# Softmax division moved from the attention weights to the attention outputs, with the reciprocals turned through DRAM

## The chip, the core and the metric

The kernel runs on one core of a Trainium2 chip. The core has five engines with one instruction queue each: TensorE (PE in the profile; its weight loads are listed apart as PEld), VectorE (DVE), ScalarE (ACT), GpSimd (POOL) and SyncE (SP), which here only starts DMAs. The metric is the device time of one execution in microseconds (us). Lower is better. Times of a kernel are medians of several runs; the profile is of one execution of its own.

## What is computed

The reference is one encoder layer over 1024 prompt tokens and, with the same weights, 512 sample tokens: RMS norm, neighbourhood attention, residual, RMS norm, a SwiGLU block, residual, final RMS norm. The change lies in the attention, which cut to what matters is:

```python
# per query row r, for each of 4 column blocks of 16 queries (x 8 rows in the kernel)
s = einsum('bjqhd,bkjchd->bhjqkc', qr, kr) * scale        # 16 heads of 64
s = where(valid, s + bias, -inf)
p = softmax(s)                                            # over the keys of the window
o = einsum('bhjqkc,bkjchd->bjqhd', p, vr)
y = o @ w_o
```

Softmax is exp(s - max) divided by the sum of these over the keys. The division can be done on the weights p, before they are multiplied with the values v, or on the outputs o, after it: the sum belongs to a query and a head, and the product with v is linear.

## The kernel before

Everything is float32. A product of two operands a and b is made of three TensorE passes over two-part splits (high part in a reduced format, low part the remainder), so each operand is cast once on ACT (`split`, L141) and its remainder subtracted on DVE (L142, or L144 and L145 where a scale is applied).

The attention runs over 8 head pairs. For the prompt a head pair takes 4 *steps* (two groups of 512 queries, two halves of each), for the sample 2 steps: 32 steps and then 16. A step works on two column blocks u = 0, 1 of 128 queries each and on both heads h of the pair. Function `step` (L477) traces its parts in this order:

1. `scores` (L391): for each block, 6 TensorE matmuls into two PSUM tiles `pss` (L397); on DVE the bias is added and the maximum taken (L405, `mx`); on ACT exp with the sum over keys as a side result `sm` (L408). DVE then takes the reciprocal `ri` (L410), and the weights `s`, 128 queries on the partitions by 384 keys (256 in the sample), are scaled by it: for h = 0 on DVE (L412), for h = 1 on ACT (L414).
2. `fill(0)`: a piece of other TensorE work, the projections of q and k for the next head pair (`pg`, L335) and, in the sample stage, pieces of the output projection (`pgo`, L593).
3. For the step before: `weighted` (L431, `po`, L434) multiplies the transposed weights `pT` with v, keys being contracted; the result lies with the 64 head dimensions on the partitions and the queries along the free axis. `collect` (L438) adds the two parts of the result, which lie in different partitions and columns of PSUM: a copy on ACT (L444) and two additions on DVE (L445, L447), the last of which writes `oT`. When both halves of a group are there, GpSimd's queue stores `oT` to DRAM (`o_d`, L462).
4. `flip` (L418), for each block: TensorE transposes the weights (`ptt`, L423) so that the keys lie on the partitions, ACT casts them to `pT` (L426), DVE subtracts for the low part (L427). After each, another `fill`.

After a step come up to two *chores* (class `Chores`, L166): a chore takes a raw tile that was loaded earlier (`rpool`, 2 buffers of tag `raw`), splits it with ACT and DVE, and starts the next load. The raw tiles are values (`vr`, four DMAs on SP's queue each, L381), weights of q and k (`wr`, L150), and later attention outputs. Bias tiles `b` (3 buffers) are filled two ahead: a memset on GpSimd (L207, L211) and DMAs on SP (L208, L209, L212, L213; L218 in the sample stage).

The order on each engine's queue is made at compile time by a planner: it takes instructions by their place in the program, but only those that its cost model holds ready at that time, so that an engine's order can differ from the program's. At run time each queue runs in order and waits at its head.

PSUM tiles of tag `S` (4 buffers) are shared by scores, transposes and others; tag `V` (2 buffers) holds `po`. Pool `apool` (L328) has 2 buffers for a tag unless it is said otherwise.

Of the kernel before, what the change touches and what calls it, by code (L numbers as in the profile page):

```python
# [11 lines left out]
F32 = mybir.dt.float32  # L12
F32R = mybir.dt.float32r
AF = mybir.ActivationFunctionType
ALU = mybir.AluOpType
# [3 lines left out]
P = 128  # L19
# [7 lines left out]
HP = H // 2  # L27
HD = 64
# [27 lines left out]
def body(tc, xp, xs, g_mix, g_ffn, g_fin, w_qkv, rpb, w_o, w_g, w_u, w_d, yp, ys):  # L56
    nc = tc.nc
# [8 lines left out]
    with es:  # L66
        cpool = es.enter_context(tc.tile_pool(name="cpool", bufs=1))
        stat = es.enter_context(tc.tile_pool(name="stat", bufs=4))
        ps = es.enter_context(tc.tile_pool(name="ps", bufs=2, space=PSUM))
        dr = es.enter_context(tc.tile_pool(name="dr", bufs=1, space=DRAM))  # L70
# [4 lines left out]

        v_d = [dr.tile([T, D // 2], F32, name=f"v_d{n}") for n in range(2)]
        o_d = dr.tile([HP, P, T], F32, name="o_d")
        x1_d = dr.tile([T, D], F32, name="x1_d")
        t_d = dr.tile([3, H, 16, 15, 32], F32, name="t_d")
        ti_d = dr.tile([3, H, 16, 15, 32], F32, name="ti_d")  # L80
# [29 lines left out]
        def psum(tag, name):  # L110
            return ps.tile([P, 512], F32, tag=tag, name=name, bufs=4 if tag == "S" else 2)
# [54 lines left out]
        class Chores:  # L166
# [7 lines left out]
            def fill(self):  # L174
                while self.jobs and len(self.loaded) < 2:
                    load, work = self.jobs.pop(0)
                    self.loaded.append((load(), work))
# [8 lines left out]
        def pool(name, **kw):  # L186
            cm = tc.tile_pool(name=name, **kw)
            return cm, cm.__enter__()
# [56 lines left out]
        with tc.tile_pool(name="vpool", bufs=2) as vp:  # L245
# [53 lines left out]
            for t in range(NT):  # L299
                if t + 2 < NT:  # L300
                    norm_tile(t + 2)
                if t == 0:
                    for td in (t_d, ti_d):
                        nc.sync.dma_start(
                            out=td.rearrange("k h i r c -> (k h i) (r c)").rearrange("(a p) f -> p a f", p=P),
                            in_=fill.rearrange("p (a f) -> p a f", a=1).to_broadcast([P, 6, 480]))
# [5 lines left out]
                if t == 8:  # L312
# [4 lines left out]
                              in_=t_d.rearrange("k h i r c -> (k h i) r c")[:, 3:11, :])  # L317
            for t in range(NT):
                v_tile(1, t, wv)
                q = t // 3  # L320
                half, src, st, n, dst = ((0, t_d, 7 - q, 8, es_d), (0, ti_d, 3 - q, 12, in_d),
                                         (4, t_d, 3 - q, 8, es_d))[t % 3]
                nc.gpsimd.dma_start(out=dst[:, :, half + q].rearrange("k h i f -> (k h) i f"),
                                    in_=src[:, :, :, st:st + n, :].rearrange("k h i r c -> (k h) i (r c)"))
# [3 lines left out]
        a_cm, ap = pool("apool", bufs=2, reuse_waits="tile")  # L328
# [59 lines left out]
            split(rv, vv[:, :, 0:4:3, :], vv[:, :, 1:3, :])  # L388
            return v

        def scores(q, k, krow, nrow, j, bias):  # L391
            n = nrow * 32
            pss = [psum("S", "pss") for _ in range(2)]
            for i, (a, b) in enumerate(PASS):
                for h, pt in enumerate(pss):
                    kv = k[h * HD:(h + 1) * HD, b].rearrange("p (r c) -> p r c", c=GW)
                    nc.tensor.matmul(pt[:, :n], q[h * HD:(h + 1) * HD, a, j].rearrange("p r i -> p (r i)"),  # L397
                                     kv[:, krow:krow + nrow, BS[j]:BS[j] + 32],
                                     start=(i == 0), stop=(i == 2))
            yield  # L400
            out = []
            for h, pt in enumerate(pss):
                s = ap.tile([P, 384], F32, tag="s", name="s", bufs=4)
                mx = stat.tile([P, 1], F32, tag="mx", name="mx")
                nc.vector.tensor_tensor_reduce(s[:, :n], pt[:, :n], bias(h), -1.0, 3.0e38,  # L405
                                               ALU.add, ALU.min, accum_out=mx)
                sm = stat.tile([P, 1], F32, tag="sm", name="sm")
                nc.scalar.activation(s[:, :n], s[:, :n], AF.Exp, bias=mx, scale=-1.0, accum_out=sm)  # L408
                ri = stat.tile([P, 1], F32, tag="ri", name="ri")
                nc.vector.reciprocal(ri, sm)  # L410
                if h == 0:
                    nc.vector.tensor_scalar(s[:, :n], s[:, :n], ri, None, ALU.mult)  # L412
                else:
                    nc.scalar.mul(s[:, :n], s[:, :n], ri)  # L414
                out.append(s)
            yield out

        def flip(ss, n):  # L418
            out = []
            for s in ss:  # L420
                pt = psum("S", "ptt")
                for c in range(n):
                    nc.tensor.transpose(pt[:, c * P:(c + 1) * P], s[:, c * P:(c + 1) * P], ident)  # L423
                pT = ap.tile([P, 3, 2, P], F32R, tag="pT", name="pT", bufs=4)
                pv = pt[:, :n * P].rearrange("p (c q) -> p c q", q=P)
                nc.scalar.copy(pT[:, :n, 0], pv)  # L426
                nc.vector.tensor_tensor(pT[:, :n, 1], pv, f32(pT[:, :n, 0]), ALU.subtract)  # L427
                out.append(pT)
            return out

        def weighted(pT, vs, j, n, pos, g):  # L431
            for h in range(2):
                for c in range(n):
                    nc.tensor.matmul(pos[h][:, g * 256:(g + 1) * 256], vs[c][:, j, h * P:(h + 1) * P],  # L434
                                     pT[h][:, c].rearrange("p z q -> p (z q)"),
                                     start=(c == 0), stop=(c == n - 1))

        def collect(pos, dst):  # L438
            for h in range(2):
                m, o = (0, HD) if h == 0 else (HD, 0)  # L440
                pv = pos[h].rearrange("p (g z q) -> p g z q", g=2, z=2)
                tmp = ap.tile([P, 2, P], F32, tag="tmp", name="tmp")
                t = tmp[m:m + HD]
                nc.scalar.copy(t, pv[o:o + HD, :, 0])  # L444
                nc.vector.tensor_tensor(t, t, pv[m:m + HD, :, 0], ALU.add)  # L445
                tv = t.rearrange("p g (r i) -> p g r i", i=16)
                nc.vector.tensor_tensor(dst(h), tv, pv[m:m + HD, :, 1].rearrange("p g (r i) -> p g r i", i=16),  # L447
                                        ALU.add)

        def steps(hp, g, q, k, v, n, store):  # L450

            oT = ap.tile([P, 512], F32, tag="o", name="oT", bufs=2)
            ov = oT.rearrange("p (r j i) -> p j r i", r=8, j=NJ)
            b = None
            for jj in range(2):
                sc = []
                for j in (jj * 2, jj * 2 + 1):
                    if j != 2:
                        b = next_bias()
                    sc.append(lambda b=b, j=j: scores(q, k, 4 * (g == 1), 4 * n, j, lambda h: b[:, h, :n * P]))  # L460
                yield dict(s=sc, n=n, jj=jj, v=v, dst=lambda h, jj=jj: ov[h * HD:(h + 1) * HD, jj * 2:jj * 2 + 2],
                           done=(lambda: nc.gpsimd.dma_start(out=o_d[hp, :, g * 512:(g + 1) * 512], in_=oT))  # L462
                           if jj else None)
                fill_bias()
# [10 lines left out]
        prev = []  # L475

        def step(st, fill):  # L477

            sc = [x() for x in st["s"]] if st else []
            for x in sc:  # L480
                next(x)
            ss = [next(x) for x in sc]
            fill(0)
            if prev:
                p, pT = prev.pop()
                pos = [psum("V", "po") for _ in range(2)]
                for u in range(2):
                    weighted(pT[u], [x() for x in p["v"]], p["jj"] * 2 + u, p["n"], pos, u)
                collect(pos, p["dst"])
                if p["done"]:  # L490
                    p["done"]()
            pT = []
            for u, x in enumerate(ss):
                pT.append(flip(x, st["n"]))
                fill(1 + u)
            if st:
                prev.append((st, pT))

        def drain(fillers):
            while fillers:  # L500
# [38 lines left out]
        for hp in range(HP):  # L539
# [5 lines left out]
            q0, q1, k = qk  # L545
# [10 lines left out]
            i = 0  # L556
# [56 lines left out]
        for hp in range(HP):  # L613
# [5 lines left out]
            n = len(jobs[hp])  # L619
# [323 lines left out]
        rt_cm, rt = pool("rt", bufs=1, side="right", reuse_waits="tile")  # L943
# [74 lines left out]
        def x_tile(tt, half, d, tag="c", bufs=15):  # L1018
            t = rows(tt, half)
            x = lt.tile([P, 512], F32, tag=tag, name=tag, bufs=bufs)  # L1020
            nc.gpsimd.dma_start(out=x, in_=x1_d[t * P:(t + 1) * P, d * 512:(d + 1) * 512])
            return x
# [28 lines left out]
        for q in range(84):  # L1051
            m, tt, h = q // 12, q % 12 // 2, q % 2
            n = SEQ[m]
# [8 lines left out]
            a, b = HALF[h]  # L1062
# [16 lines left out]
            elif n == 5:  # L1079
# [4 lines left out]
                x = x_tile(tt, 1, 0, "x", 2)  # L1084
# [45 lines left out]
```

## Time and profile before

| | |
|---|---|
| median of three runs | 1830.18 us (1823.91 to 1831.17) |
| the profiled execution | 1828.39 us, of which the span from first to last instruction is 1826.6 us |
| granted TensorE clock, mean | 0.987 |
| steps of the prompt attention | from 180 us into the span to about 517 us |
| steps of the sample attention | from 517 us to about 728 us |
| then the rest of the output projection and the SwiGLU block | to 1826.6 us |

The profile names a line of the kernel, the engine, the operation, what is written from what (`out<-in`), the count, and what ended idle time before an instruction (`<-`). A busy PE is not PE at its peak, since matmuls are pipelined and their ends are modelled. The rows that carry the argument are quoted where they are used.

### The profile page before, as it was taken

How to read it: one execution, taken by the hardware profiler on the slowest of the kernel's cores; microseconds unless marked ns; L12 is line 12 of the kernel's file. 1: busy time of each engine (PE TensorE's matmuls, PEld its weight loads, DVE VectorE, ACT ScalarE, POOL GpSimd, SP SyncE). 2: the span in 40 equal slices, each digit the busy share in tenths (PEclk: the TensorE clock that was granted, in tenths of full speed). 3: DMA queues.
4: the chain of work that ended last, by engine and by line, in shares of the span. 5: the costliest groups of instructions: out<-in, count | busy, mean ns of one | idle time of the engine just before them, and what ended most of it. 6: DMA issues, size and time to landing. Idle time of an engine off the chain costs nothing.

```text
span 1826.6 us, 25898 instructions
## 1 busy us (share of the span) xinstructions
PE 1755.7 (96%) x9178; PEld 1534.0 (84%) x9178; DVE 1222.2 (67%) x2263; ACT 869.9 (48%) x1742; POOL 441.4 (24%) x513
## 2 busy tenths in 40 slices
PE   7999999999999999999998999899999999999998
PEld 6887777777767878889998999899999988888886
DVE  4401887777887666667777877999777756546643
ACT  4411776767785554543443435433444435433423
POOL 1121000000130000103323343575424252005300
PEclk9999999999999999999999999899999999999999
DMA  7754333333465443643552635788343259645633
GB/s 242 220 187 157 108 108 101 104 117 108 125 203 155 139 145 121 196 162 120 173 167 93 209 107 168 257 295 287 112 136 122 78 191 322 194 153 165 215 103 107
DMA packets 229858, 295.60 MB, mean 162 GB/s; under 512 B 27648, under 2 KB 173824, under 8 KB 229728
## 3 DMA queue, kind: packets, MB, share of 16 engines
q1 hardware_dynamic: 205744, 215.94, 39.0%
q0 software_dynamic: 21248, 69.62, 10.4%
q10 hardware_dynamic: 2736, 8.39, 1.4%
q8 instruction: 72, 1.18, 0.3%
q14 instruction: 58, 0.48, 0.1%
HBM read 218.45 MB, written 87.97 MB: 168 GB/s over the span
## 4 chain that ended last, share of the span: by engine, by line
PE 69%; DVE 10%; DMA 9%; ACT 4%; issue 4%; POOL 2%; SPq 2%; DVEq 0%; ACTq 0%; POOLq 0%
PE pd L1066 17%; PE pa L822 15%; PE pg L335 8%; PE pd L822 7%; PE pgv L281 6%; PE pgo L593 5%; DMA vr<-v_d 4%; PE pb L822 4%; PE pss L397 3%; PE po L434 2%; PE ptt L423 2%; SPq L381 2%; DMA t<-ffn_w_down 1%; DMA wr<-na_w_qkv 1%; ACT s L408 1%
## 5 line engine op out<-in xcount | busy, mean ns | idle before, releaser
L1066 PE MATMUL pd<-wd,go 128*128 128x512 f32 x1386 | 324.7, 396 | 4.1 <-DVE wd L142 3.4
L1066 PEld LDWEIGHTS pd<-wd,go 128*128 128x128 f32 x1386 | 260.6, 188 | 68.0 <-DVE wd L142 4.8
L822 PE MATMUL pa<-h,ws 128*128 128x384 f32 x1056 | 202.9, 340 | 13.1 <-ACT c L847 10.7
L335 PE MATMUL pg<-hTp,whl 128*128 128x512 f32 x768 | 203.5, 409 | 0.0
L822 PEld LDWEIGHTS pa<-h,ws 128*128 128x128 f32 x1056 | 187.0, 191 | 16.4 <-ACT c L847 12.7
L822 PE MATMUL pd<-h,ws 128*128 128x384 f32 x1056 | 198.9, 336 | 0.1
L822 PEld LDWEIGHTS pd<-h,ws 128*128 128x128 f32 x1056 | 185.9, 189 | 0.5 <-ACT c L851 0.5
L142 DVE TENSOR_TENSOR ws<-wt,ws 128x1024 fp32r<-128x1024 f32 x88 | 114.7, 1304 | 96.7 <-ACT ws L141 96.5
L335 PEld LDWEIGHTS pg<-hTp,whl 128*128 128x128 f32 x768 | 140.4, 192 | 34.5 <-issue 7.7
L822 PE MATMUL pa<-h,wa 128*128 128x384 f32 x792 | 151.5, 344 | 9.3 <-DVE c L854 9.2
L822 PEld LDWEIGHTS pa<-h,wa 128*128 128x128 f32 x792 | 141.9, 192 | 12.3 <-DVE c L854 11.7
L593 PE MATMUL pgo<-wo,oh 128*128 128x512 f32 x576 | 138.9, 392 | 1.3 <-DVE oh L142 1.3
L141 ACT CAST go<-gr 128x768 fp32r<-128x768 f32 x84 | 65.6, 782 | 150.7 <-PE pd L1066 112.4
L408 ACT ACTIVATE s<-s,mx 128x384 f32<-128x384 f32 (+1 forms) x192 | 109.1, 570 | 54.3 <-DVE mx L405 54.1
L142 DVE TENSOR_TENSOR wa<-wr,wa 128x512 fp32r<-128x512 f32 x132 | 123.6, 948 | 11.5 <-ACT wa L141 10.4
L142 DVE TENSOR_TENSOR go<-gr,go 128x768 fp32r<-128x768 f32 x84 | 81.5, 971 | 71.6 <-ACT go L141 70.2
L894 POOL DMA_DIRECT2D gop_d<-c x66 | 50.6, 766 | 320.8 <-DVE c L885 315.9
L593 PEld LDWEIGHTS pgo<-wo,oh 128*128 128x128 f32 x576 | 107.4, 188 | 24.3 <-DVE oh L142 1.8
L141 ACT CAST wa<-wr 128x512 fp32r<-128x512 f32 x132 | 81.8, 621 | 92.4 <-PE pb L822 45.2
L141 ACT CAST ws<-wt 128x1024 fp32r<-128x1024 f32 x88 | 92.5, 1052 | 68.6 <-issue 47.0
L335 PE MATMUL pg<-hTs,whl 128*128 128x512 f32 x384 | 105.7, 411 | 1.6 <-DVE q L346 1.6
L822 PE MATMUL pb<-h,wa 128*128 128x384 f32 x528 | 101.3, 340 | 4.3 <-ACT wa L141 4.1
(159 smaller groups left out, 2954.4 us busy)
## 6 DMA issues: line engine op xcount, KB each, us to landing
wr<-ffn_w_gate SPq DMA_DIRECT2D x44, 512.0 KB
wr<-ffn_w_up SPq DMA_DIRECT2D x44, 512.0 KB
wr<-na_w_qkv SPq DMA_DIRECT2D x38, 512.0 KB
gop_d<-gs POOLq DMA_DIRECT2D x88, 192.0 KB, 5.8
gr<-gop_d SPq DMA_DIRECT2D x42, 384.0 KB
gr<-gop_d SPq DMA_DIRECT2D x42, 320.0 KB
gop_d<-c POOLq DMA_DIRECT2D x66, 192.0 KB, 2.5
vr<-v_d SPq DMA_DIRECT2D x192, 64.0 KB
```

Of the source, the lines that this page charges most:

```text
L141: nc.scalar.copy(hi, raw)
L142: nc.vector.tensor_tensor(lo, raw, f32(hi), ALU.subtract)
L281: nc.tensor.matmul(pg, hh[a][:, k, c:c + P], wv[k // 2][b][:, k % 2], start=(k == 0 and i == 0), stop=(k == KB - 1 and i == 2))
L335: nc.tensor.matmul(pg, w[:, a, k, :], h[b][:, k, c:c + 512], start=(k == 0 and i == 0), stop=(k == KB - 1 and i == 2))
L381: nc.sync.dma_start(out=raw[:, j * P:(j + 1) * P], in_=src[:, BS[j]:BS[j] + 32, :])
L397: nc.tensor.matmul(pt[:, :n], q[h * HD:(h + 1) * HD, a, j].rearrange("p r i -> p (r i)"), kv[:, krow:krow + nrow, BS[j]:BS[j] + 32], start ...
L408: nc.scalar.activation(s[:, :n], s[:, :n], AF.Exp, bias=mx, scale=-1.0, accum_out=sm)
L423: nc.tensor.transpose(pt[:, c * P:(c + 1) * P], s[:, c * P:(c + 1) * P], ident)
L593: nc.tensor.matmul(pg, ohs[k // 4][:, a, k % 4], wo[:, b, k, n * 512:(n + 1) * 512], start=(k == 0 and i == 0), stop=(k == KB - 1 and i == 2))
L822: nc.tensor.matmul(bank[:, :HT], a(y, k), b[:, z, k], start=start and k == 0 and i == 0, stop=k == KB // 2 - 1 and i == 2, skip_group_chec ...
L894: nc.gpsimd.dma_start(out=gop_d[i, 3 * c:3 * c + 3, :, p].rearrange("j q t -> q j t"), in_=a.rearrange("q (j t) -> q j t", j=3))
L1066: nc.tensor.matmul(pd, go[:, y, i - a], wds[m, i][:, z], start=(i == 0 and k == 0), stop=(i == NP - 1 and k == 2))
```

## The change

The weights are no longer scaled. The four sums of a step (two blocks, two heads) are written by the four exps into the columns of one tile `sm` of 128 x 4. The new function `reciprocals` takes one reciprocal of that tile on DVE, stores it by SP's queue to a slot of a new DRAM buffer `ri_d` with the queries as the innermost axis, and reads it back by two DMAs on the same queue, each repeating the same 2 x 128 numbers of one head over 64 partitions, into a tile `rt` whose layout is that of the outputs. `collect` now leaves the sum of the parts in one tile `tmp` (one buffer), and GpSimd multiplies it with `rt` of the same step and writes `oT`.

```diff
-        def scores(q, k, krow, nrow, j, bias):
+        def scores(q, k, krow, nrow, j, bias, sm):
...
-                sm = stat.tile([P, 1], F32, tag="sm", name="sm")
-                nc.scalar.activation(s[:, :n], s[:, :n], AF.Exp, bias=mx, scale=-1.0, accum_out=sm)
-                ri = stat.tile([P, 1], F32, tag="ri", name="ri")
-                nc.vector.reciprocal(ri, sm)
-                if h == 0:
-                    nc.vector.tensor_scalar(s[:, :n], s[:, :n], ri, None, ALU.mult)
-                else:
-                    nc.scalar.mul(s[:, :n], s[:, :n], ri)
+                nc.scalar.activation(s[:, :n], s[:, :n], AF.Exp, bias=mx, scale=-1.0, accum_out=sm[:, h:h + 1])
...
-        def collect(pos, dst):
+        def reciprocals(sm, slot):
+
+            ri = stat.tile([P, 4], F32, tag="ri", name="ri")
+            nc.vector.reciprocal(ri, sm)
+            nc.sync.dma_start(out=ri_d[slot].rearrange("u h q -> q (u h)"), in_=ri)
+            rt = ap.tile([P, 2, P], F32, tag="rt", name="rt")
+            for h in range(2):
+                nc.sync.dma_start(out=rt[h * HD:(h + 1) * HD],
+                                  in_=ri_d[slot, :, h].rearrange("(o u) q -> o u q", o=1).to_broadcast([HD, 2, P]))
+            return rt
+
+        def collect(pos, dst, rt):
+            tmp = ap.tile([P, 2, P], F32, tag="tmp", name="tmp", bufs=1)
             for h in range(2):
                 m, o = (0, HD) if h == 0 else (HD, 0)
                 pv = pos[h].rearrange("p (g z q) -> p g z q", g=2, z=2)
-                tmp = ap.tile([P, 2, P], F32, tag="tmp", name="tmp")
                 t = tmp[m:m + HD]
                 nc.scalar.copy(t, pv[o:o + HD, :, 0])
                 nc.vector.tensor_tensor(t, t, pv[m:m + HD, :, 0], ALU.add)
-                tv = t.rearrange("p g (r i) -> p g r i", i=16)
-                nc.vector.tensor_tensor(dst(h), tv, pv[m:m + HD, :, 1].rearrange("p g (r i) -> p g r i", i=16),
-                                        ALU.add)
+                nc.vector.tensor_tensor(t, t, pv[m:m + HD, :, 1], ALU.add)
+            nc.gpsimd.tensor_tensor(dst, tmp.rearrange("p g (r i) -> p g r i", i=16),
+                                    rt.rearrange("p g (r i) -> p g r i", i=16), ALU.mult)
...
         def step(st, fill):
 
-            sc = [x() for x in st["s"]] if st else []
+            sm = stat.tile([P, 4], F32, tag="sm", name="sm") if st else None
+            sc = [x(sm[:, u * 2:u * 2 + 2]) for u, x in enumerate(st["s"])] if st else []
             for x in sc:
                 next(x)
             ss = [next(x) for x in sc]
+            rt = reciprocals(sm, st["slot"]) if st else None
             fill(0)
             if prev:
-                p, pT = prev.pop()
+                p, pT, r = prev.pop()
...
-                collect(pos, p["dst"])
+                collect(pos, p["dst"], r)
...
             if st:
-                prev.append((st, pT))
+                prev.append((st, pT, rt))
```

In `steps` the destination becomes one view of `oT` for both heads, and each step is given its slot of `ri_d` (48 slots of 2 x 2 x 128).

More of the change, by code (lines that the diff above doesn't have):

```diff
@@ L77, in body @@
         o_d = dr.tile([HP, P, T], F32, name="o_d")
+        ri_d = dr.tile([HP * 6, 2, 2, P], F32, name="ri_d")
         x1_d = dr.tile([T, D], F32, name="x1_d")
@@ L459, in steps @@
                         b = next_bias()
-                    sc.append(lambda b=b, j=j: scores(q, k, 4 * (g == 1), 4 * n, j, lambda h: b[:, h, :n * P]))
-                yield dict(s=sc, n=n, jj=jj, v=v, dst=lambda h, jj=jj: ov[h * HD:(h + 1) * HD, jj * 2:jj * 2 + 2],
+                    sc.append(lambda sm, b=b, j=j: scores(q, k, 4 * (g == 1), 4 * n, j, lambda h: b[:, h, :n * P], sm))
+                yield dict(s=sc, n=n, jj=jj, v=v, dst=ov[:, jj * 2:jj * 2 + 2], slot=hp * 6 + g * 2 + jj,
                            done=(lambda: nc.gpsimd.dma_start(out=o_d[hp, :, g * 512:(g + 1) * 512], in_=oT))
```

## The prediction

> **What bounds the kernel now.** I read the page's busy times first, then busy times by stretch for the attention, then the waits of TensorE there, then the chain of work that ended last and the order of time.
>
> ```profile
> PE 1755.7 (96%) x9178; PEld 1534.0 (84%) x9178; DVE 1222.2 (67%) x2263; ACT 869.9 (48%) x1742; POOL 441.4 (24%) x513
> ...
> 180.00:511.00 331.00, 320.56 (x1842) 255.43 (x1841) 266.24 (x762) 236.17 (x580) 29.55 (x62) 0.99 0.38 111
> 511.00:730.00 219.00, 209.06 (x1128) 167.71 (x1128) 150.93 (x442) 126.41 (x333) 27.10 (x27) 0.99 0.49 151
> ```
>
> The columns of the last two rows are: stretch, its length, busy time of PE, PEld, DVE, ACT and POOL, clock, DMA share, GB/s. PE is busy 96% overall and in both attention stages. The change touches only these 550 us, and PE is idle there for 10.4 and 9.9 us. But a pipelined matmul that is held up counts as busy, so I also price the steps by their pace.
>
> ```profile
> 244.23 2.98 PE pg L335 x12
> 254.40 2.99 PE pg L335 x12
> ...
> L397 PE MATMUL pss<-kp,q x384: 334/338/447, 180.2 to 510.8; 64*128 64x384 f32 x192
> L335 PE MATMUL pg<-hTs,whl x384: 387/394/702, 478.7 to 704.8; 128*128 128x512 f32 x192
> L397 PE MATMUL pss<-ks,q x192: 276/280/387, 517.2 to 715.6; 64*128 64x256 f32 x192
> ```
>
> The first two rows (the chain in order of time) are the same point of two successive unhindered prompt steps: 10.17 us. The others give first and last starts. The 28 steps of head pairs 0 to 6 run from 180.2 to 478.7, 10.66 us each, so 13.7 us are lost. The last prompt pair fills each step with 12 projection matmuls instead of 24: TensorE needs 4 x (10.17 - 2.98) = 28.8 us, but the stage takes 517.2 - 478.7 = 38.5, so 9.7 are lost. What takes over there shows in two 20-us stretches, beside a later one:
>
> ```profile
> 500.00:520.00 20.00, 19.47 (x110) 14.97 (x110) 18.11 (x51) 17.13 (x40) 3.46 (x3) 1.00 0.64 203
> 520.00:540.00 20.00, 17.61 (x95) 13.04 (x94) 18.33 (x50) 15.65 (x40) 8.96 (x5) 1.00 0.73 239
> ...
> 600.00:620.00 20.00, 20.00 (x113) 16.26 (x112) 13.54 (x37) 10.67 (x26) 1.08 (x2) 1.00 0.52 157
> ```
>
> Around the change of stage DVE is over 90% busy: DVE and ACT set the pace of some eight steps. From 600 us on, output projection fills TensorE (20.00 of 20) and little is left to win.
>
> **The change part by part.**
>
> *Removed.* Groups by line, one scaling of the sample from the order of time, and the waits of PE:
>
> ```profile
> L412 DVE TENSOR_SCALAR s<-s,ri 128x384 f32<-128x384 f32 (+1 forms) x96 | 39.7, 414 | 0.7
> L410 DVE RECIPROCAL ri<-sm 128x1 f32<-128x1 f32 x192 | 28.9, 157 | 18.5 <-ACT s L408 16.2
> L414 ACT ACTIVATE s<-s,ri 128x384 f32<-128x384 f32 (+1 forms) x96 | 52.8, 570 | 12.9 <-DVE ri L410 12.8
> ...
> 526.21 0.34 DVE L412 TENSOR_SCALAR s<-s,ri 128x256 f32<-128x256 f32 x1
> ...
> PE pss L397 <- DVE pT L427: 5.4, 7, 0.9
> PE ptt L423 <- DVE s L412: 4.8, 5, 1.4
> PE ptt L423 <- ACT s L414: 4.4, 13, 1.1
> ```
>
> A step loses two scalings on DVE (2 x 0.41) and three of four reciprocals (3 x 0.157; the one left has four columns, taken at the same price): 1.3 us of DVE, and 2 x 0.57 = 1.14 us of ACT. Over 48 steps that is about 61 us of DVE and 53 of ACT. Most of it hides under TensorE. What can reach the end is the transposes' wait for scaled weights (4.8 + 4.4) and the scores' wait for `pT` (5.4), plus the pace lost above. By stage:
>
> - Head pairs 0 to 6: the chain leaves TensorE for detours like this (time, length, what):
>
> ```profile
> 223.94 0.99 ACT s L408 x4
> 225.13 0.79 ACT s L408 x3
> 225.92 1.01 ACT s L414 x2
> ...
> 231.11 0.61 DVE v L142
> 231.77 0.54 SPq L381
> 233.49 4.48 DMA vr<-v_d
> ...
> 450.11 3.77 DMA vr<-v_d
> ```
>
> ACT and DVE run late, so a raw buffer is freed late, so SP starts the next value load late, so ACT stands waiting for it. From the one at 233 to the one at 450 us the chain holds nine such loads; each loses the 1.0 us of L414: 9 of the 13.7 us at best.
> - Last prompt pair: four steps on DVE's pace, 4 x 1.3 = 5.2 us.
> - First four sample steps: DVE saves 2 x 0.34 + 0.47 = 1.15 us each (0.34 by the row at 526.21), 4.6 us.
> - Later sample steps: TensorE is full; 0.
>
> *Added on DVE and TensorE:* nothing. The additions of `collect` stay at their 0.42 us. *The one buffer `tmp`:* ACT's copy of the next step waits for the multiplication of this one, some 10 us earlier; hidden.
>
> *Added on GpSimd:* 48 multiplications of 128x256. None is in the trace; nearest are
>
> ```profile
> L889 POOL TENSOR_TENSOR gs<-c 128x384 f32<-128x384 f32 x22 | 23.1, 1048 | 41.2 <-DVE c L885 41.2
> L891 POOL TENSOR_TENSOR gs<-c 128x384 f32<-128x384 f32 x22 | 31.9, 1451 | 0.0
> ```
>
> Two thirds of these by size: 0.70 to 0.97 us; I take 0.75. GpSimd is busy 57 us of 550, so it has room. Behind the multiplication on its queue stand the bias memsets and the store of `oT`; the memsets wait for DVE's next scores anyway. `rt` has a whole step to arrive. Hidden; at the end of the stage the output projection covers 1 us.
>
> But GpSimd and DVE hold each other up:
>
> ```profile
> 523.33 2.40 POOL L517 TENSOR_TENSOR wo<-or,wo 128x1024 fp32r<-128x1024 f32 x1
> 523.70 2.59 DVE L142 TENSOR_TENSOR v<-vr,v 128x512 fp32r<-128x512 f32 x1
> ...
> 481.42 4.94 POOL L517 TENSOR_TENSOR wo<-oraw,wo 128x1024 fp32r<-128x1024 f32 x2 [8.81 <-ACT wo L516]
> 484.32 2.26 DVE L412 TENSOR_SCALAR s<-s,ri 128x384 f32<-128x384 f32 x1
> ```
>
> The split of v, with both inputs in SBUF, took 2.59 us and ended 0.56 after GpSimd's did, and the scaling took 2.26 in place of 0.41. So the change takes one victim away (1.8 us at 484) and sends 48 new holds of 0.75 us. The Trainium skill, "SBUF — State Buffer", section "Who interferes with whom", says that a DVE instruction with two SBUF inputs contends with a GpSimd one that reads SBUF and that the second to issue blocks until the first finishes; the trace agrees with the 2.59 us. After `collect` DVE does four `pT` subtractions from PSUM, 0.5 us each, and the multiplication falls beside these. I count 0; a price if the cover fails is rival 3.
>
> *Added on SP:* per step a store of 512 separate 4-byte numbers and two loads of 128 rows of 512 bytes; the loads must wait until the store has landed, and SP stands there meanwhile.
>
> ```profile
> L381 SPq DMA_DIRECT2D vr<-v_d x192: 509/521/2246, 93.0 to 691.8; - x192
> L311 SPq DMA_DIRECT2D t_d<-na_rpb x48: 532/606/2022, 19.1 to 64.3; - x48
> q1 hardware_dynamic: 13474, 5.61, 54.2%
> DMA to landing us min/median/max: 2.2/2.3/4.7
> ```
>
> Issue costs 0.52 (a `vr` load is the same shape as an `rt` load) and 0.61 for the store, by L311's pieces of 64 bytes. The third row is SP's DMA queue from 20 to 66 us, mostly those pieces: 0.542 x 46 us x 16 engines / 13474 = 30 ns a packet, so 512 packets on 16 engines take about 1 us. Landing: 2.2 to 4.7 us (the store of `oT`); I take 2.5. SP is thus held 0.6 + 2.5 + 1.0 = 4.1 us in a step, 3.8 to 6.3 by the ends. Today a prompt head pair issues 30 loads of about 0.55 us, 16 of its 41 us, so SP isn't full (33 of 41). What matters is who stands behind: the value and weight loads, which are on the chain. They are earlier in the program, so the planner lets them go first when their buffer is free; it is freed by splits in the middle of the scores or at the step's end, while the store becomes ready after the fourth exp. So I take that a chained load meets the 0.6 us store, not the wait: 9 x 0.6 = 5 us in the prompt, 2 more in the sample.
>
> *Sum:* -9 - 5.2 - 4.6 - 1.8 (the hold at 484) + 5 + 2 = -13.6; part of the freed time will be taken by what is late next (casts of q and k, splits of v), so I take three quarters: -10. From 1828.4 that is 1818.4; the median shown is 1.8 higher, so a median of 1820 would be the same gain. I say **1819**.
>
> **Rivals.**
>
> 1. *Hidden (no change).* TensorE is 96 to 97% busy in both stages. If only the direct waits of the transposes (9.2 us) shrink by half and SP gives it back, the time is 1825 to 1832.
>
> For the next one, value loads on the chain in the sample, first and last of nine with two between, and the row of ACT's waits for them:
>
> ```profile
> 555.83 3.88 DMA vr<-v_d
> ...
> 640.48 4.91 DMA vr<-v_d
> ...
> 655.50 4.26 DMA vr<-v_d
> ...
> 691.81 5.17 DMA vr<-v_d
> ...
> L141 ACT CAST v<-vr 128x512 fp32r<-128x512 f32 x46 | 28.6, 627 | 45.1 <-DMA vr<-v_d 44.8
> ```
>
> 2. *SP's wait takes the place (slower).* If the planner puts store, wait and both loads ahead of the value load, that load starts 4.1 us later and gains 1.0 back: +3.1. The chain holds nine such loads in the prompt and as many in the sample, where SP, ACT and TensorE already turn in one loop of 15.0 us (640.48 to 655.50). At 18 loads it is +56, at a third of them +18: 1838 to 1860, likeliest 1846. It decides from a delay of 1.0 us a load on. For it: ACT waited 44.8 us for these loads, and there are only two raw buffers. Against it: the priorities above, and SP's free time in the prompt.
> 3. *GpSimd holds DVE.* If each multiplication meets a split, DVE loses 48 x 0.75 = 36 us, more than half of what it saved; on the detours and the DVE-paced steps (about 17) it costs 17 x 0.75 = 13: 1828 to 1836. The rows show such a hold only beside GpSimd operations of 2.4 us and more. This is the case that the rule of the Trainium skill's "SBUF — State Buffer", named above, would bring about.
>
> **How the numbers follow.** The forecast gets 0.55, rival 1 0.15, rival 2 0.24, rival 3 0.06. The forecast's own range is 1808 to 1828: above, all of SP's price and half of the gain; below, pace lost in the detours wholly regained (13.7 instead of 9) and no price of SP. Half a per cent, 9.2 us from 1830.2, is about what a measurement of this kernel can tell from no change, so faster means under 1821: three quarters of the forecast, 0.41. The rest of the forecast (0.14), rival 1 and half of rival 3 make 0.32 the same, rival 2 and the other half 0.27 slower. Leaving out the upper half of rival 2 and a tail below, the range is 1808 to 1846.
>
> **What would show it.** Right: the waits of `ptt` for `s` nearly gone, DVE's busy time in 180 to 730 us down by about 55 us and ACT's by about 50, the first sample scores some 8 us earlier, `rt` never last before GpSimd's multiplication. Rival 2: SP's waits for the landing of `ri_d` in front of L381's loads, and ACT's wait for `vr` well above 45 us. Rival 3: splits of v above 1 us beside multiplications. The forecast is wrong if the planner's order on TensorE changes so that other waits grow, or if the 4-byte store takes many us to land.

## The result and the profile after

| | median us (runs) | against before |
|---|---|---|
| before | 1827.39 (4: 1823.91 to 1831.17) | 1 |
| after | 2070.23 (4: 2069.20 to 2086.61) | 1.1352, 95% interval 1.1312 to 1.1391 |

The changed kernel is 13.5% slower, far outside the range. (A fourth run of before has joined the three of the first table. The ratio is worked out from the single runs, so it can differ a little from the quotient of two medians, here 1.133.) The page of after (span, busy times, granted clock in 40 slices, then the chain that ended last, by engine and by line):

```profile
span 2069.0 us, 26084 instructions
...
PE 1827.7 (88%) x9178; PEld 1584.1 (77%) x9178; DVE 1179.6 (57%) x2023; ACT 824.7 (40%) x1646; POOL 474.4 (23%) x561
...
PEclk9999888888887888889999999999999999999999
...
PE 54%; DMA 23%; DVE 7%; issue 6%; SPq 4%; ACT 3%; POOL 2%; ACTq 0%; POOLq 0%; DVEq 0%
PE pd L1073 15%; PE pa L829 14%; DMA ri_d<-ri 10%; PE pd L829 7%; DMA vr<-v_d 6%; PE pgv L282 5%; PE pg L336 4%; PE pb L829 4%; SPq L382 2%; PE pgo L600 2%; DMA t<-ffn_w_down 1%; DMA wr<-na_w_qkv 1%; SPq L439 1%; PE pss L398 1%; ACT s L408 1%
```

The work that was to go is gone: DVE is busy 42.6 us less, ACT 45.2 us less. But the store of the reciprocals (`ri_d<-ri`) is now 10% of the chain, over 200 us, where the prediction charged 7 us in all for what is added on SP's queue. The granted clock drops in the slices of the attention and is at 0.9 or more again behind them. First and last starts of the score matmuls, and busy times by stretch (columns as in the prediction):

```profile
L398 PE MATMUL pss<-kp,q x384: 334/442/686, 180.1 to 643.1; 64*128 64x384 f32 x192
L398 PE MATMUL pss<-ks,q x192: 276/383/580, 657.5 to 948.4; 64*128 64x256 f32 x192
```

```profile
0.00:180.00 180.00, 169.19 (x770) 137.51 (x770) 48.94 (x65) 55.40 (x91) 31.40 (x60) 1.00 0.67 204
...
583.00:657.00 74.00, 45.39 (x215) 35.22 (x214) 31.56 (x79) 29.58 (x69) 11.11 (x13) 0.75 0.41 99
180.00:975.00 795.00, 606.51 (x2995) 477.69 (x2996) 375.27 (x964) 317.00 (x815) 88.53 (x136) 0.85 0.41 96
```

Up to 180 us nothing has changed (TensorE is busy 169.4 us there before, 169.2 after). The prompt's steps take 477 us up to the first sample scores (337 before), the sample's last scores begin 291 us after its first (198 before). TensorE works at a granted clock of 0.85 there, and at 0.75 in its emptiest stretch; a matmul's own time grows with it, as the groups by line show, of after:

```profile
L336 PE MATMUL pg<-hTp,whl 128*128 128x512 f32 x768 | 220.0, 435 | 0.0
```

and of before:

```profile
L335 PE MATMUL pg<-hTp,whl 128*128 128x512 f32 x768 | 203.5, 409 | 0.0
```

SP's order of time in one step (start, length, line, operation) shows where the time goes:

```profile
300.56 0.60 SPq L213 DMA_DIRECT2D bp<-in_d  x1
301.21 0.61 SPq L214 DMA_DIRECT2D bp<-es_d  x1
301.91 0.53 SPq L436 DMA_DIRECT2D ri_d<-ri  x1
313.42 1.23 SPq L439 DMA_DIRECT2D rt<-ri_d  x2
314.75 0.55 SPq L382 DMA_DIRECT2D vr<-v_d  x1
```

The store is issued in 0.53 us. Then SP starts nothing for 10.98 us, until the store has landed; the value load that ACT needs comes third behind it. Over all 48 steps the gap from the end of the store's issue to the first load has a minimum of 7.84, a median of 9.1 and a maximum of 11.57 us (worked out from SP's order of time); below it is called *the gap*. What the 16 DMA engines moved in the middle of that gap (305.5 to 313.3 us):

```profile
DMA packets 26, 0.01 MB, mean 1 GB/s; under 512 B 25, under 2 KB 25, under 8 KB 25
```

The store's small packets are on record ahead of that. These are the windows 301.9 to 304 and 304 to 306 us, with 158 and 426 packets under 512 bytes, for 512 numbers:

```profile
DMA packets 656, 0.60 MB, mean 283 GB/s; under 512 B 158, under 2 KB 610, under 8 KB 656
...
DMA packets 479, 0.12 MB, mean 58 GB/s; under 512 B 426, under 2 KB 461, under 8 KB 479
```

So the packets are through within some 4 us, then next to nothing moves, and the store still has not landed for 7 us more: its landing is limited neither by bandwidth nor by packets that the records show. The waits of 180 to 975 us (who waited for whom: us, times, longest), first SP's, then the engines':

```profile
SPq L439 <- DMA ri_d<-ri: 360.6, 48, 10.9
```

```profile
ACT v L142 <- DMA vr<-v_d: 223.9, 34, 11.6
DVE v L143 <- ACT v L142: 144.7, 18, 10.6
...
POOL oT L452 <- DMA rt<-ri_d: 110.1, 15, 12.8
...
PE pss L398 <- DVE pT L421: 103.8, 32, 9.7
...
PE ptt L417 <- ACT s L408: 35.7, 7, 12.9
```

On average SP waits 7.5 us a step for the landing (360.6 / 48). ACT's wait for values is 223.9 us where it was 44.8. From there, as the rows suggest, the delay goes on to DVE's part of the split, to `pT` behind it on DVE's queue, and to TensorE's scores.

### The profile page after: what moved, and what is told of

The parts are those of the page before. It is cut to its first block, busy times and chain, and to the rows that moved or that the text cites. A ratio compares the mean times of both kernels' runs of the same rounds, so it can differ in the third digit from the quotient of the medians.

```text
span 2069.0 us, 26084 instructions
## 1 busy us (share of the span) xinstructions
PE 1827.7 (88%) x9178; PEld 1584.1 (77%) x9178; DVE 1179.6 (57%) x2023; ACT 824.7 (40%) x1646; POOL 474.4 (23%) x561
## 4 chain that ended last, share of the span: by engine, by line
PE 54%; DMA 23%; DVE 7%; issue 6%; SPq 4%; ACT 3%; POOL 2%; ACTq 0%; POOLq 0%; DVEq 0%
PE pd L1073 15%; PE pa L829 14%; DMA ri_d<-ri 10%; PE pd L829 7%; DMA vr<-v_d 6%; PE pgv L282 5%; PE pg L336 4%; PE pb L829 4%; SPq L382 2%; PE pgo L600 2%; DMA t<-ffn_w_down 1%; DMA wr<-na_w_qkv 1%; SPq L439 1%; PE pss L398 1%; ACT s L408 1%
## 5 line engine op out<-in xcount | busy, mean ns | idle before, releaser
L336 PE MATMUL pg<-hTp,whl 128*128 128x512 f32 x768 | 220.0, 435 | 0.0
L336 PEld LDWEIGHTS pg<-hTp,whl 128*128 128x128 f32 x768 | 153.3, 209 | 40.9 <-issue 9.8
L600 PE MATMUL pgo<-wo,oh 128*128 128x512 f32 x576 | 145.6, 404 | 12.3 <-DVE xo L604 10.7
L398 PE MATMUL pss<-kp,q 64*128 64x384 f32 x384 | 73.0, 446 | 87.6 <-DVE pT L421 87.0
L452 POOL TENSOR_TENSOR oT<-tmp,rt 128x256 f32<-128x256 f32 x48 | 35.6, 742 | 432.4 <-DVE tmp L451 295.9
L336 PE MATMUL pg<-hTs,whl 128*128 128x512 f32 x384 | 129.2, 480 | 4.2 <-ACT whl L145 4.2
L398 PEld LDWEIGHTS pss<-kp,q 64*128 64x128 f32 x384 | 45.7, 228 | 114.0 <-DVE pT L421 104.7
```

The lines of the kernel that those rows point to most:

```text
L336: nc.tensor.matmul(pg, w[:, a, k, :], h[b][:, k, c:c + 512], start=(k == 0 and i == 0), stop=(k == KB - 1 and i == 2))
L452: nc.gpsimd.tensor_tensor(dst, tmp.rearrange("p g (r i) -> p g r i", i=16), rt.rearrange("p g (r i) -> p g r i", i=16), ALU.mult)
L600: nc.tensor.matmul(pg, ohs[k // 4][:, a, k % 4], wo[:, b, k, n * 512:(n + 1) * 512], start=(k == 0 and i == 0), stop=(k == KB - 1 and i == 2))
```

## The experiments

The theory after the result: the 4-byte store into DRAM lands some 9 us late, SP stands at the head of its queue meanwhile, and the loads behind it are late. Rivals: the store also slows the DMA engines for everyone; or the loss comes from elsewhere in the change (GpSimd's multiplications, the single `tmp`, a new order on TensorE). In what follows "the turn" is the store of the reciprocals with the two loads that read them back. Ratios are against runs of the kernel before on the same chip (1822.7 to 1825.6 us).

### Parts alone: the turn, and all but the turn

`e3_turn_only` is the kernel before, scalings and all, with the turn added; nothing reads `rt`.

```diff
+            ri = stat.tile([P, 4], F32, tag="ri4", name="ri4")
+            nc.vector.reciprocal(ri, sm)
+            nc.sync.dma_start(out=ri_d[slot].rearrange("u h q -> q (u h)"), in_=ri)
+            rt = ap.tile([P, 2, P], F32, tag="rt", name="rt", bufs=1)
...
+                nc.sync.dma_start(out=rt[h * HD:(h + 1) * HD],
```

> The kernel before, which still scales its weights, with the turn added: one more reciprocal of 128x4, the store and the two loads of each step, read by nobody. Theory (SP's wait is the cost): 2040 to 2110, as much as the whole change or a little more, since ACT and DVE do more. Rival (the cost is in what uses the result): 1828 to 1850.

`e2_no_turn` is the changed kernel without the store and the loads; GpSimd multiplies by a constant tile of ones, so the division is left out.

```diff
-            nc.sync.dma_start(out=ri_d[slot].rearrange("u h q -> q (u h)"), in_=ri)
...
-            return rt
+            return ones
```

> The kernel after without the store and the loads: GpSimd multiplies with a constant tile of ones, so the division by the sums is left out. Theory (the turn alone costs): 1805 to 1825, which is the gain of 10 to 20 us that the forecast had without SP's price. Rival (multiplication on GpSimd or the order of work costs): above 1840.

Measured: e3 2072.11 us, ratio 1.1372 (1.1347 to 1.1396), gap 9.3 us: as slow as after. e2 1805.11 us, ratio 0.9905 (0.9888 to 0.9922). So the whole loss is in the turn, and without it the change is a gain of about 17 us (0.95% of 1827). GpSimd's multiplications, the single `tmp` and the new order on TensorE are all in e2 and none is in e3, so they are not the cause by themselves. With the turn in place, the work taken off DVE and ACT buys nothing that shows: e3 still does all the scalings, and its interval overlaps that of after. e2's profile: the page, one tile's first and last starts, groups of the new and the disputed instruction with min/median/max in ns, and the waits of 180 to 705 us:

```profile
PE 1747.8 (97%) x9178; PEld 1532.3 (85%) x9178; DVE 1181.0 (65%) x2023; ACT 825.5 (46%) x1646; POOL 474.6 (26%) x562
```

```profile
L400 PE MATMUL pss<-ks,q x192: 277/282/389, 506.8 to 697.1; 64*128 64x256 f32 x192
...
L449 POOL TENSOR_TENSOR oT<-tmp,ones x48: 723/737/747, 197.8 to 709.4; 128x256 f32<-128x256 f32 x48
...
L145 DVE TENSOR_TENSOR v<-vr,v x48: 676/693/2358, 169.6 to 678.1; 128x512 fp32r<-128x512 f32 x48
```

```profile
ACT v L144 <- DMA vr<-v_d: 41.9, 26, 4.1
...
PE pss L400 <- DVE pT L423: 3.6, 5, 1.1
...
PE ptt L419 <- ACT s L410: 0.2, 1, 0.2
```

The sample's scores begin 10.4 us earlier than before (506.8 against 517.2) and the stage is 8.1 us shorter (190.3 against 198.4). The transposes no longer wait for weights (0.2 us against 9.2), and a multiplication takes 0.74 us.

### Is it SP's wait alone?

`e1_late` issues the two loads of `rt` one step later, when the store has long landed (a dependency added in the source keeps the planner from taking them earlier); the store stays where it was. `f2_act_store` is e1 with the store on ACT's queue. `g5_store_only` is e2 with the store and no loads: nothing in the kernel waits for it.

```diff
-            rt = reciprocals(sm, st["slot"]) if st else None
+            if st:
+                reciprocals(sm, st["slot"])
...
-                collect(pos, p["dst"], r)
+                collect(pos, p["dst"], turned(p["slot"]))
```

> The kernel after, but each pair of rt loads is placed on SP's queue one step later, behind the next step's store; the same DMAs, no wait for a store that was just issued. Theory (SP stands 8 to 11 us a step for the landing of the store of 4-byte pieces, and the value loads stand behind it): the waits of the rt loads for ri_d fall from 311 us to under 30, ACT's wait for vr from 224 to about 45, time 1810 to 1835. Rival (the loss is in the division on the outputs itself, GpSimd's multiplication or the changed order on TensorE): time stays above 2000.

```diff
-            nc.sync.dma_start(out=ri_d[slot].rearrange("u h q -> q (u h)"), in_=ri)
+            nc.scalar.dma_start(out=ri_d[slot].rearrange("u h q -> q (u h)"), in_=ri)
```

> As e1_late, the store on ACT's queue, the loads on SP's. If the store of 4-byte pieces holds up only the loads behind it on its own queue: 1810 to 1840, the moved bytes per second while a store is out as high as before it, ACT's wait for vr about 45 us. If it holds up the DMA engines themselves, whatever queue the loads are on: 1950 to 2040.

```diff
+            nc.sync.dma_start(out=ri_d[slot].rearrange("u h q -> q (u h)"), in_=ri)
             return ones
```

> As e2_no_turn (multiplied by ones, so without the division), with the store of 4-byte pieces on SP and no loads of it: nothing waits for its landing. If the store holds up the loads queued behind it: 1930 to 2000, near e1_late. If the waiting for it is the only cost: 1805 to 1815.

Measured: e1 2004.05 us, ratio 1.1000 (1.0980 to 1.1020); f2 1990.43 us, 1.0908 (1.0863 to 1.0952); g5 1985.46 us, 1.0892 (1.0859 to 1.0924). Taking the wait away returned a third of the loss at most, so the theory that SP's wait is the cost, for which 1810 to 1835 was expected of e1, does not hold. (e1's time is above 2000, as its rival said, but not for the rival's reason: e2 has the division on the outputs and is fast.) The bare store costs 0.0892 + 0.0095 = 0.099 of the time, about 180 us or 3.8 us a step, with nobody waiting for it. ACT's wait for values in g5, 180 to 900 us, beside 41.9 in e2:

```profile
ACT v L144 <- DMA vr<-v_d: 155.4, 32, 10.5
```

In e1 SP goes on at once, and this is its order of time in one step:

```profile
262.75 0.42 SPq L436 DMA_DIRECT2D ri_d<-ri  x1
263.22 0.55 SPq L382 DMA_DIRECT2D vr<-v_d  x1
263.86 1.26 SPq L442 DMA_DIRECT2D rt<-ri_d  x2
265.17 1.12 SPq L382 DMA_DIRECT2D vr<-v_d  x2
```

but what it starts crawls. The DMA engines of e1 in three windows, 262.7 to 264, 266 to 272 and 272 to 274 us:

```profile
DMA packets 379, 0.27 MB, mean 206 GB/s; under 512 B 174, under 2 KB 379, under 8 KB 379
...
DMA packets 609, 0.30 MB, mean 49 GB/s; under 512 B 33, under 2 KB 609, under 8 KB 609
...
DMA packets 813, 0.42 MB, mean 208 GB/s; under 512 B 2, under 2 KB 813, under 8 KB 813
```

206 GB/s as the store begins, 49 while it lands, 208 at once when it is through (the chain of e1 has this store from 262.75 for 9.85 us). So the store holds up other transfers too. It does so across queues: `oT` goes out on GpSimd's queue, and its median time to landing is 9.4 us in e1 (2.3 before), and 7.5 us in g5 (2.6 in e2). The row of e1:

```profile
o_d<-oT POOLq DMA_DIRECT2D x24, 256.0 KB, 9.4
```

In f2, with the store on ACT's queue, SP's value loads are nearly as late as in e1 (the engines' waits of f2, then of e1):

```profile
ACT v L142 <- DMA vr<-v_d: 124.2, 25, 10.6
```

```profile
POOL oT L457 <- DMA rt<-ri_d: 506.9, 38, 26.7
...
ACT v L142 <- DMA vr<-v_d: 143.2, 27, 11.2
```

The Trainium skill, "DMA: Bandwidth & Descriptors", section "Issuing engines are not separate DMA queues", says that DMAs of all issuing engines end on the same 16 DMA engines and interleave there; f2's ratio, within 0.01 of e1's, agrees that another queue is no way out.

### What of the store is slow: pieces, their number, or where they fall

The store is 512 pieces of 4 bytes, 4 bytes apart in DRAM (neighbouring addresses come from neighbouring queries, which lie in different partitions). Five variants take its properties apart. `e4_rows16` writes each query's four numbers as one piece of 16 bytes (128 pieces); `f1_spaced` keeps 512 pieces of 4 bytes but puts them 64 bytes apart; `g3_spaced16` puts them 16 bytes apart; `h2_rows16_pieces` uses e4's addresses, but its source numbers lie 8 bytes apart in SBUF, so that they stay 512 pieces of 4 bytes, four in a row from one query. In f1 and g3 too the four numbers of a query follow each other in DRAM, so h2 is the variant to compare them with: only the distance differs there. `f4_rows16_late` is e4 with e1's late loads.

The store of e4, f4 and h2:

```diff
-            nc.sync.dma_start(out=ri_d[slot].rearrange("u h q -> q (u h)"), in_=ri)
+            nc.sync.dma_start(out=ri_d[slot].rearrange("u h q -> (u h q)").rearrange("(q c) -> q c", c=4), in_=ri)
```

in h2 with its source

```diff
-            ri = stat.tile([P, 4], F32, tag="ri", name="ri")
+            ri = stat.tile([P, 8], F32, tag="ri", name="ri").rearrange("p (c e) -> p c e", e=2)[:, :, 0]
```

and the store of f1 (in g3 with `e=4`):

```diff
-            nc.sync.dma_start(out=ri_d[slot].rearrange("u h q -> q (u h)"), in_=ri)
+            nc.sync.dma_start(out=ri_d[slot].rearrange("(q c e) -> q c e", c=4, e=16)[:, :, 0], in_=ri)
```

> The kernel after, the store writing each query's four numbers as one piece of 16 bytes, 128 pieces instead of 512, the loads unchanged in shape (so that the numbers that multiply the outputs stand in another order). If the landing time goes with the number of small pieces: the gap from store to load falls from 8 to 11 us to 3 to 4.5, time 1850 to 1930. If it comes from what stands ahead in the queue or from a fixed delay of any small store: gap and time stay, 8 us and 2040 to 2090.

> The kernel after, each of the 512 numbers of a store written 64 bytes from the next in a larger buffer (filled with ones before the attention; the loads read 2 x 2 x 128 numbers of the same slot, in the same shape, so that the outputs are multiplied by other numbers). If neighbouring 4-byte writes to the same stretch of DRAM make the landing long: gap from store to load 3 to 4.5 us and a time of 1830 to 1860. If it is the number of pieces, wherever they go: gap 8 to 11 us, 2040 to 2100.

> As f1_spaced, 16 bytes from number to number in place of 64: 512 pieces of 4 bytes, four in each 64 bytes. If the landing grows with the pieces in a stretch of 64 bytes (16 in the kernel after: 9.1 us, 1 in f1: 2.7 us): a gap of 3.5 to 6 us, 1850 to 1930. If only writes that touch each other are slow: as f1, 2.7 us, 1835 to 1845.

> As e4_rows16 in its addresses (each query's four numbers side by side, the outputs multiplied by other numbers), but the numbers lie 8 bytes apart in SBUF, so that the store is 512 pieces of 4 bytes again, 16 in each 64 bytes of DRAM, from four queries. If the number of writes in a stretch decides: gap 8 to 11 us, 2040 to 2090, as the kernel after. If it is the number of partitions that write one stretch (16 there, 4 here): 3 to 5 us, 1835 to 1890.

> e4_rows16 with the loads one step later (the outputs are multiplied by other numbers, as there). If what is left in e4 over the kernel without a turn (31 us) is SP's wait of 71 us for the landing: 1806 to 1818. If it is the 128 pieces of 16 bytes in the queue: 1825 to 1840.

| store | pieces | from piece to piece in DRAM | gap us min/median/max | us | ratio (95%) |
|---|---|---|---|---|---|
| after | 512 of 4 B | 4 B | 7.84/9.1/11.57 | 2070.23 | 1.1352 (1.1312 to 1.1391) |
| h2 | 512 of 4 B | 4 B | 6.77/9.4/12.3 | 2088.78 | 1.1443 (1.1410 to 1.1476) |
| g3 | 512 of 4 B | 16 B | 3.13/3.69/6.51 | 1867.84 | 1.0246 (1.0216 to 1.0277) |
| f1 | 512 of 4 B | 64 B | 2.11/2.7/5.63 | 1838.58 | 1.0078 (1.0054 to 1.0103) |
| e4 | 128 of 16 B | 16 B | 1.11/3.05/5.39 | 1835.75 | 1.0075 (1.0050 to 1.0099) |
| f4 | 128 of 16 B | 16 B | loads late | 1827.24 | 1.0017 (1.0001 to 1.0033) |

SP's waits for the landing follow: in h2

```profile
SPq L439 <- DMA ri_d<-ri: 365.9, 48, 12.1
```

and in e4

```profile
SPq L439 <- DMA ri_d<-ri: 71.3, 41, 3.2
```

f1 has all 512 pieces of 4 bytes and lands in a third of the time: neither the number of pieces nor their size makes the landing long. h2 has e4's addresses, four neighbours from one query, and is no faster than after: who writes the neighbours does not matter, only that they are separate pieces. What decides is how close separate pieces lie in DRAM. Counted in stretches of 64 bytes: 16 pieces 9.1 us, 4 pieces 3.7, 1 piece 2.7; each further piece costs (9.1 - 3.7) / 12 = 0.45 us and (3.7 - 2.7) / 3 = 0.33 us. That looks like pieces of one stretch being written one after the other. But the length of the stretch wasn't varied by itself, nor was the distance apart from the extent of the whole store (2, 8 and 32 KB), and which part of the path does it, DMA engine or memory, no record shows: that stays open.

A landing of 3 us is not free either. f1 and e4 are still 0.017 above e2, some 31 us, and slower than the kernel before: the short landing costs more than the whole gain. SP's waits for the landing and ACT's for values (41.9 in e2), of f1 from 160 to 740 us:

```profile
SPq L444 <- DMA ri_d<-ri: 62.7, 39, 3.3
```

```profile
ACT v L144 <- DMA vr<-v_d: 70.8, 26, 7.3
```

f4 regained only 8.5 of e4's 30 us over e2 (0.006 of 0.017 by the ratios), less than expected if SP's wait were all of it. In f4 GpSimd's multiplications wait for `rt`, which comes a step late:

```profile
POOL oT L457 <- DMA rt<-ri_d: 237.3, 28, 13.9
```

Whether that wait costs time was not tested in f4. f3 below has late loads too, and a store of four rows of 512 bytes in another place; it has a ratio of 0.9966, 0.005 below f4's, so part of the rest may lie in the 16-byte pieces. The price was not taken apart further.

### Turning the reciprocals before they are stored

TensorE has unused columns in the first tile `ptt` of a step's `flip`. In `f3_pe_turn` it transposes the 128 x 4 reciprocals into them, ACT copies the 4 x 128 result out, and the store has four pieces of 512 bytes; the loads come late as in e1. `g1_pe_turn_early` starts the loads at the beginning of the next step, `g2_pe_turn_pool` is g1 with all three DMAs on GpSimd's queue.

```diff
             for s in ss:
                 pt = psum("S", "ptt")
...
+                if ri is not None and s is ss[0]:
+                    nc.tensor.transpose(pt[:4, 3 * P:], ri, ident)
+                    rr = stat.tile([4, P], F32, tag="rr", name="rr", bufs=1)
+                    nc.scalar.copy(rr, pt[:4, 3 * P:])
+                    nc.sync.dma_start(out=ri_d[slot].rearrange("u h q -> (u h) q"), in_=rr)
```

> As e1_late, the reciprocals turned by a 128x4 transpose on TensorE into unused columns of the first PSUM tile of the weights' transposes, copied by ACT and stored as four pieces of 512 bytes; one buffer for rt. If the 4-byte pieces are the whole cost: no long landing, 1806 to 1818, faster than the kernel before. If any turn through DRAM costs on SP's queue: 1825 to 1845.

> As f3_pe_turn, the loads of rt traced at the start of the next step instead of just ahead of its collect. f3's multiplications waited 183 us for rt, and ACT's copies for the one tmp behind them. If that holds the chain: 1808 to 1815 where f3 had 1819. If the chain is elsewhere (three more DMAs a step on SP's queue beside the value loads): 1816 to 1822, as f3.

> As g1, with the store of four rows and the two loads on GpSimd's queue. If SP's queue is what is left of the price: 1806 to 1813. If it is not, or if the loads hold up the bias memsets behind them on GpSimd's queue: 1815 to 1830.

Measured: f3 1818.91 us, ratio 0.9966 (0.9951 to 0.9980); g1 1818.62 us, 0.9978 (0.9965 to 0.9992); g2 1831.68 us, 1.0050 (1.0034 to 1.0067). The loss is gone, but f3 has only a third of e2's gain and lies just above the 1818 of its first expectation. TensorE's waits in f3 name something new:

```profile
PE ptt L419 <- DVE ri L440: 6.8, 7, 1.5
```

The first flip now waits for the reciprocal, which waits for the last of four exps. Fetching `rt` earlier, in g1, changed nothing: GpSimd waited 176.9 us for `rt` in f3 and 4.4 in g1 (180 to 700 us), so that wait was covered (GpSimd's wait for `tmp` rose from 45.1 to 227.6 instead), and TensorE's wait for `ri` stayed (10.1 us). In g2 GpSimd itself stands waiting, for ACT's copy and for the store's landing, and holds its memsets and multiplications:

```profile
POOL ri_d L422 <- ACT rr L421: 120.9, 31, 6.0
...
POOL rt L447 <- DMA ri_d<-rr: 39.9, 24, 4.8
```

So the transpose was moved to the second block's flip, with late loads (`h3_pe_turn_second_late`) and with loads behind the next scores (`h1_pe_turn_second`):

```diff
-                pT.append(flip(x, st["n"], *((ri, st["slot"]) if u == 0 else ())))
+                pT.append(flip(x, st["n"], *((ri, st["slot"]) if u == 1 else ())))
```

> As f3, the transpose of the reciprocals in the second block's flip. If TensorE's wait for ri (6.8 us in f3) is what it loses: 1811 to 1816. If it is GpSimd's wait for rt with one tmp behind it: 1818 to 1826.

> As g1, the transpose of the reciprocals in the second block's flip and the loads traced behind the next step's scores. TensorE's wait of 10 us for ri goes. If that wait cost the end: 1808 to 1815. If SP now stands for the store's landing, since store and loads come close together on its queue: 1818 to 1830.

h3 measured 1809.79 us (6 runs, 1808.61 to 1813.59), ratio 0.9918 (0.9902 to 0.9934); h1 1816.44 us, 0.9958 (0.9941 to 0.9976), whose loads wait at SP's head for the landing again (76.1 us in all). h3 is faster than both kernels, than before by 0.8%, and TensorE's waits in it have no row for `ri`. Its sample scores and its prompt stretch:

```profile
L398 PE MATMUL pss<-ks,q x192: 276/280/389, 508.7 to 699.8; 64*128 64x256 f32 x192
```

```profile
180.00:511.00 331.00, 327.24 (x1925) 263.56 (x1925) 243.12 (x620) 215.78 (x562) 52.51 (x94) 0.99 0.45 129
```

TensorE is busy 327.2 of these 331 us, where it was 320.6 before, and the sample's scores begin within 1.9 us of e2's. Most of the gain that the change has without a turn (ratio 0.9905) is kept by this one.

## Why the prediction was wrong, point by point

- **The step that failed** is "Landing: 2.2 to 4.7 us (the store of `oT`); I take 2.5", with the "about 1 us" for 512 packets beside it. Measured: 9.1 us, about twice the upper end, and the packets were on record over some 4 us. Both rows it came from were of larger pieces (L311's 64 bytes; `oT`'s long rows). Spaced by 64 bytes the same pieces do land in 2.7 us, so the 2.5 was right for such a store and wrong for this one. Of the property that mattered, many pieces close together, the trace of before had no row; the bounds should have said so, and reached further up.
- **What no step had:** that a store would hold up other transfers on the DMA engines. It is the larger part. From e2 to g5 the ratio rises by 0.099 (store alone); from g5 to after by 0.046 (the wait at SP's head and the loads).
- **"A chained load meets the 0.6 us store, not the wait"** failed as well. In the step at 301.91 us the store and both loads stand ahead of the value loads; of the four prompt steps with a store from 260 to 302 us, two had all four value loads behind them. This matters even with the landing that was assumed: f1 lands in 2.7 us and e4 in 3.05, and they are 31 us above e2, where the sum had 5 + 2. With such a store the time would have been 1836 to 1839, inside the stated range but slower than before, at the lower end of rival 2. (Not all of these 31 us is SP's wait: taking it away, in f4, gave back 0.006 of 0.017.) Without the wait the loads still crawl in the kernel as it is (e1).
- **Rival 2** had the right sign and place, and the right mechanism for the smaller part of the loss: SP's waits for `ri_d` ahead of the value loads, ACT's wait for `vr` at 223.9 us, as the prediction's last part said it would show. Its price was the failed step's. Its own sum for 18 loads, 1828.4 + 56, is 1884, above the 1860 that it gave as its top. With the 4.7 us of the upper bound a load starts 6.3 us later and gains 1.0: 18 x 5.3 = 95, or 1924. With the measured 9.1 us SP is held 0.6 + 9.1 + 1.0 = 10.7 us; 18 x 9.7 = 175, or some 2003 us, still 67 short of 2070. And the experiments share the loss out otherwise: about 180 us for the store that nobody waits for, 84 (0.046) for the wait and the loads.
- **The gain** was right where it could be seen, without the turn: the sum without SP's price was -20.6 us (three quarters of it 15), e2 measured -17 (ratio 0.9888 to 0.9922, so 14 to 20 us). The first sample scores came 10.4 us earlier, forecast 8. By stage it was less in the prompt (10.4 of 16.0, the terms 9, 5.2 and 1.8) and more in the sample (8.1 against 4.6): "Later sample steps: TensorE is full; 0" was too low. Busy time fell by 41 us on DVE and 44 on ACT in e2, not by 55 and 50. Summed over the groups by line it fell by 57 and 52; instructions on one engine overlap in the trace, and busy time counts the overlap once.
- **GpSimd:** 0.75 us taken, 0.74 measured, hidden in e2. **Rival 3** is not seen in e2: the split of v has a median of 0.693 us, and its whole is 48 x (0.778 - 0.726) = 2.5 us more than before (means of the groups by line), of 36 at stake.
- **The clock:** a lower granted clock was not forecast. How much of the loss is its own was not measured. It goes with the waits: 0.85 where TensorE is busy 76% of the time (606.51 of 795) and 0.75 where it is 61% (45.39 of 74); the profiles of e4 and f1 have means of 0.983 and 0.985, that of after 0.932.

## What to carry to other kernels

Before a turn through DRAM is priced, ask how many separate pieces fall next to each other there, not how many bytes move: 2 KB in 4-byte pieces cost 9 us and slowed everyone's transfers meanwhile, while four rows of 512 bytes, turned first on TensorE in columns that stood empty, kept most of the gain. An operation with no row of its own needs an upper bound from an unlike row, and a rival with that operation in it belongs inside the range. To tell a wait from its cause, run the transfer with nobody waiting for it: here (g5) that left two thirds of the loss in place.

## What the runs showed of the hardware that was not expected

- 512 pieces of 4 bytes landed in 2.7 us (median of the gap) at 64 bytes' distance, 3.7 at 16 and 9.1 to 9.4 at 4, whichever partition the neighbours came from.
- The dense store's packets are on record within some 4 us; then the DMA engines show 26 packets in 7.8 us, and it still has not landed. While it lands, other transfers run at 49 GB/s (e1) where 206 and 208 stand before and after; a store on another queue landed in 9.4 us in place of 2.3.
- With waits of this kind the granted clock fell to 0.75 in a stretch of 74 us, and a 128x512 matmul's mean rose from 409 to 435 ns over the kernel.
